# Hybrid GLA/DSA block with a PEER mixer: the dense stage's remaining dot products spread over 122 chunks instead of 112, and weighted three chunks ahead instead of five

## The chip, the core and the metric

The kernel runs on one core of a Trainium2 chip. A NeuronCore has TensorE (PE in the profile, with PEld for its weight loads), VectorE (DVE), ScalarE (ACT), GpSimd (POOL) and SyncE (SP), which issues most of the transfers. The metric is the time of one execution on the device in microseconds (us); the median of several runs counts.

## The reference

A decoder block for 512 tokens of width 1024: two token mixers (gated linear attention and sparse latent attention), merged, and then a PEER channel mixer. Only the last one matters here. Each token has 8 heads x 16 experts out of 16384, with gates:

```python
def block(inp):
    hx, ix, gx = inp
    u = expert_u[ix]
    v = expert_v[ix]
    a = jax.nn.gelu(jnp.einsum('td,thkd->thk', hx, u).astype(jnp.float32), approximate=False) * gx
    return jnp.einsum('thk,thkd->td', a.astype(hx.dtype), v)
```

So a token's output is the sum over its 128 experts of gelu(h . u_e) x gate_e x v_e.

## The kernel before

The PEER mixer is done in two ways. For the first half of the tokens (2 blocks of 128) the rows of `u` and `v` that a token picked are fetched by indirect DMA: `gather` (POOL, line 1009) brings 128 rows per step, one per token, of 8 KB (`u` and `v` side by side) in its last part; DVE takes the dot product (`dot`, line 1014) and one step later adds the weighted `v` half to the sum (`add`, line 1023). Its tiles `grow` are a ring of four. For the other 256 tokens (`NDT`) all 16384 experts are computed, 128 chunks (`P`) of 128 experts each:

- `dots_of` (line 931) makes one chunk's *dot*: h x u for 128 experts and 256 tokens, 8 products of `projT` (line 184) that TensorE runs as 16 matmuls, then Gelu on ACT (line 943) into a slot of `kept`, a ring of 48 (`AHEAD`). A load of `u` (line 937) brings two chunks, 1 MB, into the ring `up` of two slots.
- `weigh` (line 965) multiplies a chunk by its matrix of gates (DVE, line 972), which an earlier stage built; for the first 48 chunks that has been done there. The gates come in tiles of 8 chunks (`gtile`, line 961).
- The body of `dense` (line 950) loads `v` (line 979, two chunks, 1 MB, a ring of three), calls `weigh` for the chunk `LEAD` ahead, splits the weights and `v` into a high part (ACT, line 116) and the rest (DVE, line 117), `as` in a ring of four and `vs` in a ring of two, and adds the chunk's product: 4 accumulators x 3 matmuls of 128x512 (lines 186 to 188). Chunks 126 and 127 are multiplied together. Then come the dots that are due and one step of the gather (`pump`, at a rate of 1.05 per chunk).

48 dots are made before the dense stage starts; the other 80 inside it, by the rule in line 1002. At chunk 120 the tile `fx`, for the residual, takes a slot of the ring `up` (line 981). The order within an engine is set at build time by the framework's scheduler, from the order of the program and from `pace`, the DVE instruction after which a step of the gather may be placed. Each engine and each DMA queue runs its instructions in that order.

Of the kernel before, what the change touches and what calls it, by code (L numbers as in the profile page):

```python
# [20 lines left out]
P = 128  # L21
# [18 lines left out]
NE = 7  # L40
RATE_ADA, RATE_GLA, RATE_DSA, RATE_G, RATE_DENSE = 0.4, 0.75, 0.9, 1.0, 1.05
AHEAD = 48
LEAD = 5
DOTS = (8, 16)
RATE_SEL = 3.0
GB = 16
# [13 lines left out]
def hybrid_block_kernel(ctx, tc, x, c_col, w_ada, b_ada, b_col, g1_col, g2_col, wT, wN, wM, w_br, w_o,  # L60
# [50 lines left out]
    def behind(i):  # L111

        pace[0] = i.ins

    def split(hi, lo, src, eng=None, hi_eng=None):
        (hi_eng or nc.scalar.copy)(hi, src)  # L116
        i = (eng or nc.vector).tensor_tensor(lo, src, hi.bitcast(F32), op=ALU.subtract)  # L117
        if eng is not nc.gpsimd:
            pace[0] = i.ins
# [25 lines left out]
    def pump(n=1.0):  # L145

        if quiet[0]:
            return
        for b in background:
            b[2] += n * b[1]  # L150
            while b[2] >= 1:
                b[2] -= 1
                next(b[0], None)
# [28 lines left out]
    def mm(dst, a, b, first, last, **kw):  # L182
        if len(a) == 1:
            nc.tensor.matmul(dst, a[0], b[0], start=first, stop=last, **kw)  # L184
        else:
            nc.tensor.matmul(dst, a[0], b[0], start=first, stop=False, **kw)  # L186
            nc.tensor.matmul(dst, a[0], b[1], start=False, stop=False, **kw)  # L187
            nc.tensor.matmul(dst, a[1], b[0], start=False, stop=last, **kw)  # L188
# [723 lines left out]
    def finish(Tt, x2, peer):  # L912

        y = wp.tile([P, D], F32, name="fy", tag="raw", bufs=NRAW)
        ss = dn.tile([P, 2], F32, name="fs", bufs=2)
        for n in range(2):
            ns = slice(n * 512, (n + 1) * 512)
            nc.vector.tensor_tensor(y[:, ns], peer[n], gate2[:, ns], op=ALU.mult)
            nc.vector.tensor_tensor(x2[:, ns], x2[:, ns], y[:, ns], op=ALU.add)
            nc.scalar.activation(y[:, ns], x2[:, ns], AF.Square, accum_out=ss[:, n:n + 1])  # L920
        r = dn.tile([P, 1], F32, name="fr", bufs=2)
        nc.vector.tensor_tensor(r, ss[:, 0:1], ss[:, 1:2], op=ALU.add)
        rstd_of(r, r, D, 1)
        for n in range(2):
            ns = slice(n * 512, (n + 1) * 512)
            nc.vector.scalar_tensor_tensor(y[:, ns], x2[:, ns], r, fing[:, ns], op0=ALU.mult, op1=ALU.mult)
            nc.sync.dma_start(out[Tt * P:(Tt + 1) * P, ns], y[:, ns])
# [3 lines left out]
    def dots_of(ib):  # L931

        early = dn is None
        if ib % 2 == 0:
            pool, tag, bufs = ((wp, "w2", 2), (wp, "w2", 2), (hp, "hh", 1), (hp, "hl", 1))[ib // 2 % 4] if early else (dn, "up", 2)
            up[0] = pool.tile([P, 2, D], F32, name="up", tag=tag, bufs=bufs)
            nc.sync.dma_start(up[0], u_t[ib // 2])
        p = pmm(True)
        projT(p[:, :NDT], [up[0][:, ib % 2]], h2[1])
        a = kept[:, ib % AHEAD]  # L940
        d = built[0] if ib < AHEAD else 0
        if d < NDT:
            nc.scalar.activation(a[:, d:], p[:, d:NDT], AF.Gelu)  # L943
        if d:
            t = gb.tile([P, NDT], F32, name="dg", bufs=2)[:, :d]
            nc.scalar.activation(t, p[:, :d], AF.Gelu)
            behind(nc.vector.tensor_tensor(a[:, :d], a[:, :d], t, op=ALU.mult))
        made[0] += 1

    def dense():  # L950
        banks = [psc, psc, ptr, ptr]
        acc = [[banks[2 * i + n]() for n in range(2)] for i in range(NT - NG)]
        as4 = hp.tile([P, 4, 2, NDT], F32R, name="as", tag="hh")
        gts = []

        def load_g(c):

            if c < P // 8:
                pool, tag = ((dn, "gtile"), (hp, "hl"))[c % 2]
                gts.append(pool.tile([P, NDT // GB, 8, GB], F32, name="gtile", tag=tag))  # L960
                nc.sync.dma_start(gts[-1], gd[c - AHEAD // 8])

        load_g(AHEAD // 8)

        def weigh(ib):

            if ib < AHEAD:
                return
            if ib % 8 == 0:
                load_g(ib // 8 + 1)  # L970
            a3 = kept[:, ib % AHEAD].rearrange("p (b t) -> p b t", t=GB)
            behind(nc.vector.tensor_tensor(a3, a3, gts[ib // 8 - AHEAD // 8][:, :, ib % 8], op=ALU.mult))

        late_ops = []
        vb = x2 = None
        for ib in range(P):
            if ib % 2 == 0:
                vb = dn.tile([P, 2, D], F32, name="vb", bufs=3)
                nc.sync.dma_start(vb, v_t[ib // 2])
            if ib == P - 8:  # L980
                x2 = dn.tile([P, NT - NG, D], F32, name="fx", tag="up", bufs=2)
                for i in range(NT - NG):
                    nc.sync.dma_start(x2[:, i], x2d[NG + i])
            if ib + LEAD < P:
                weigh(ib + LEAD)
            a = as4[:, ib % 4]
            v = wp.tile([P, 2, D], F32R, name="vs", tag="w2", bufs=2)
            split(a[:, 0], a[:, 1], kept[:, ib % AHEAD])
            split(v[:, 0], v[:, 1], vb[:, ib % 2])
            a, v = [[t[:, 0], t[:, 1]] for t in (a, v)]  # L990
            late_ops.append((ib, a, v))
            stage[0] = ib
            if ib == P - 2:
                continue
            for i in range(NT - NG):
                ts_ = slice(i * P, (i + 1) * P)
                for n in range(2):
                    ns = slice(n * 512, (n + 1) * 512)
                    for jb, a, v in late_ops:
                        mm(acc[i][n], [t[:, ts_] for t in a], [t[:, ns] for t in v], jb == 0, jb == P - 1)  # L1000
            late_ops.clear()
            while made[0] < AHEAD + (ib + 1) * (P - AHEAD) // (P - 16) and made[0] < P:
                dots_of(made[0])
            pump()
        for i in range(NT - NG):
            finish(NG + i, x2[:, i], acc[i])
# [137 lines left out]
    made, built = [0], [0]  # L1144
# [21 lines left out]
    nc.sync.dma_start(gate2, gated[1])  # L1166
    background[:] = [[gat, RATE_DENSE, 0.0]]
    dense()
    drain(gat)

# [66 lines left out]
```

## Time and profile before

| | |
|---|---|
| median of 3 runs | 1853.64 us (1849.02 to 1855.12) |
| profiled execution: time, span | 1861.09 us, 1859.4 us |
| TensorE busy, weight loads busy | 1725.0 us (93%), 1466.6 us (79%) |
| DVE busy | 1432.8 us (77%) |
| ACT, POOL busy | 719.0 us (39%), 540.5 us (29%) |
| moved by DMA | 573.33 MB, mean 308 GB/s |
| dense stage, first to last matmul | 1202.95 to 1847.79 us |

The span is from the first to the last instruction; the time of the same execution is 1.7 us longer. Matmuls overlap each other in the records, so TensorE's work is better read from the distance between starts than from lengths.

### The profile page before, as it was taken

The page shows a single profiled execution, that of the slowest core. Times are in us where ns is not written, and L with a number is a line of the kernel's source. Part 1 is how long each engine was busy: PE and PEld are TensorE (multiplying, and loading weights), DVE is VectorE, ACT ScalarE, POOL GpSimd, SP SyncE. Part 2 cuts the span into 40 slices and gives each one's busy share as a digit, 9 for nine tenths or more (in the row PEclk, how much of TensorE's full clock was granted, in tenths as well). Part 3 has the DMA queues.
Part 4 walks back from the last instruction along what each step waited for, and adds up shares of the span by engine and source line. Part 5 has one row for each costly group of instructions (what it writes and reads, how often), then busy time and mean ns, then how long its engine had stood idle before and what let it go on. Part 6 is the DMA issues. An engine that isn't in the chain of part 4 may idle for free.

```text
span 1859.4 us, 25034 instructions
## 1 busy us (share of the span) xinstructions
PE 1725.0 (93%) x8898; PEld 1466.6 (79%) x8898; DVE 1432.8 (77%) x2985; ACT 719.0 (39%) x1694; POOL 540.5 (29%) x459
## 2 busy tenths in 40 slices
PE   6999999989899988988999789699999999999995
PEld 3888999878667877877778678588888888888874
DVE  5797645348999868757996999388878888788887
ACT  3644465332121134102144778243333434333343
POOL 0012000001454456653431666021222222222220
PEclk9999999989998999998999889899999999999998
DMA  7757556625786799996886999699999999999983
GB/s 289 281 182 272 187 188 213 231 88 204 245 303 237 284 353 387 381 383 233 294 286 222 345 315 367 246 416 401 403 401 404 397 404 412 395 405 410 393 354 122
DMA packets 145279, 573.33 MB, mean 308 GB/s; under 512 B 14449, under 2 KB 41201, under 8 KB 111106
## 3 DMA queue, kind: packets, MB, share of 16 engines
q1 hardware_dynamic: 89858, 303.28, 44.1%
q0 software_dynamic: 55296, 268.46, 37.4%
q8 instruction: 70, 1.15, 0.2%
q14 instruction: 55, 0.45, 0.1%
HBM read 553.86 MB, written 17.83 MB: 307 GB/s over the span
## 4 chain that ended last, share of the span: by engine, by line
issue 33%; PE 29%; DVE 15%; POOL 12%; DMA 8%; ACT 2%; SPq 0%; POOLq 0%; DVEq 0%; another core or an unknown queue 0%; ACTq 0%
POOL grow L1009 11%; PE pmm L184 8%; DMA grow<-rows,ids 4%; DVE grow L1014 3%; PE pmx L184 2%; PE pmm L187 2%; PE pmm L186 2%; PE pmm L188 2%; DVE gacc L1023 2%; DMA gd<-gs 2%; PE psc L898 2%; PE ptr L898 1%; DMA adaw<-w_ada 1%; PE pmx L187 1%; PE pmx L186 1%
## 5 line engine op out<-in xcount | busy, mean ns | idle before, releaser
L1009 POOL DMA_INDIRECT grow<-rows,ids x384 | 482.9, 1258 | 838.8 <-DVE h2n L1023 451.0
L184 PE MATMUL pmm<-h2h,up 128*128 128x256 f32 x2048 | 468.4, 381 | 5.0 <-ACT kept L943 3.1
L184 PEld LDWEIGHTS pmm<-h2h,up 128*128 128x128 f32 x2048 | 385.5, 191 | 59.3 <-ACT kept L943 3.9
L1014 DVE SCALAR_TENSOR_TENSOR grow<-grow,h2n 128x1024 f32<-128x1024 f32 x256 | 310.4, 1219 | 66.5 <-DMA grow<-rows,ids 65.2
L117 DVE TENSOR_TENSOR vs<-vb,vs 128x1024 fp32r<-128x1024 f32 x128 | 156.3, 1221 | 33.1 <-ACT vs L116 32.6
L1023 DVE SCALAR_TENSOR_TENSOR gacc<-grow,dots,gacc 128x1024 f32<-128x1024 f32 x127 | 161.9, 1275 | 15.1 <-DMA grow<-rows,ids 14.0
L1023 DVE SCALAR_TENSOR_TENSOR h2n<-grow,dots,h2n 128x1024 f32<-128x1024 f32 x127 | 162.5, 1280 | 0.0
L116 ACT CAST vs<-vb 128x1024 fp32r<-128x1024 f32 x128 | 133.3, 1042 | 6.0 <-PE ptr L188 3.9
L117 DVE TENSOR_TENSOR w<-raw,w 128x1024 fp32r<-128x1024 f32 x79 | 98.0, 1240 | 45.3 <-ACT w L116 45.0
L186 PE MATMUL psc<-vs,as 128*128 128x512 f32 x256 | 114.6, 454 | 14.5 <-ACT vs L116 14.5
L187 PE MATMUL psc<-vs,as 128*128 128x512 f32 x256 | 102.7, 401 | 10.4 <-DVE vs L117 10.4
L116 ACT CAST w<-raw 128x1024 fp32r<-128x1024 f32 x79 | 82.6, 1046 | 72.9 <-PE pmm L188 32.8
L184 PE MATMUL pmm<-hh,raw 128*128 128x256 f32 x416 | 99.8, 388 | 4.3 <-DVE bsg L689 2.1
L116 ACT CAST as<-kept 128x256 fp32r<-128x256 f32 x128 | 51.3, 403 | 133.7 <-PE ptr L187 128.9
L1062 ACT ACTIVATE dots<-dots 128x1 f32<-128x1 f32 x128 | 25.8, 202 | 198.2 <-DVE grow L1014 198.1
L188 PE MATMUL psc<-vs,as 128*128 128x512 f32 x256 | 101.0, 395 | 0.0
L187 PE MATMUL ptr<-vs,as 128*128 128x512 f32 x256 | 100.6, 393 | 0.0
L188 PE MATMUL ptr<-vs,as 128*128 128x512 f32 x256 | 100.6, 393 | 0.0
L186 PE MATMUL ptr<-vs,as 128*128 128x512 f32 x256 | 99.4, 393 | 0.0
L94 POOL TENSOR_TENSOR rs<-rs,mhalf 128x1 f32<-128x1 f32 (+1 forms) x24 | 18.1, 756 | 266.5 <-DVE rs L93 266.4
L184 PEld LDWEIGHTS pmm<-hh,raw 128*128 128x128 f32 x416 | 77.9, 193 | 17.3 <-DVE bsg L689 2.5
L117 DVE TENSOR_TENSOR as<-kept,as 128x256 fp32r<-128x256 f32 x128 | 53.4, 423 | 47.0 <-ACT as L116 46.9
(377 smaller groups left out, 3527.4 us busy)
## 6 DMA issues: line engine op xcount, KB each, us to landing
up<-u_t SPq DMA_DIRECT2D x64, 1024.0 KB
vb<-v_t SPq DMA_DIRECT2D x64, 1024.0 KB
raw<-wT SPq DMA_DIRECT2D x74, 512.0 KB
adaw<-w_ada SPq DMA_DIRECT2D x20, 1024.0 KB
raw<-wN SPq DMA_DIRECT2D x32, 512.0 KB
raw<-w_br SPq DMA_DIRECT2D x32, 512.0 KB
raw<-w_pq SPq DMA_DIRECT2D x32, 512.0 KB
gd<-gs SPq DMA_DIRECT2D x16, 640.0 KB
```

The costliest lines, as they stand in the source:

```text
L94: nc.gpsimd.tensor_tensor(dst, dst, mhalf[:, :w], op=ALU.pow)
L116: (hi_eng or nc.scalar.copy)(hi, src)
L117: i = (eng or nc.vector).tensor_tensor(lo, src, hi.bitcast(F32), op=ALU.subtract)
L184: nc.tensor.matmul(dst, a[0], b[0], start=first, stop=last, **kw)
L186: nc.tensor.matmul(dst, a[0], b[0], start=first, stop=False, **kw)
L187: nc.tensor.matmul(dst, a[0], b[1], start=False, stop=False, **kw)
L188: nc.tensor.matmul(dst, a[1], b[0], start=False, stop=last, **kw)
L898: nc.tensor.matmul(p[:, t], pm[:, t4_ + t], qm[:, t4_ + t], start=True, stop=True)
L1009: nc.gpsimd.indirect_dma_start(out=dst, out_offset=None, in_=table, in_offset=bass.IndirectOffsetOnAxis(ap=index[0][:, r:r + 1], axis=0))
L1014: nc.vector.scalar_tensor_tensor(u, u, 1.0, h2n[i], op0=ALU.mult, op1=ALU.mult, accum_out=dots[i][:, r:r + 1])
L1023: nc.vector.scalar_tensor_tensor(gacc, v, w, gacc, op0=ALU.mult, op1=ALU.add)
L1062: nc.scalar.activation(w, w, AF.Gelu)
```

## The change

Two lines change. `LEAD` is 3 instead of 5: a chunk is multiplied by its gates in the iteration three before its own. The number of dots that must be made after chunk `ib` is now 48 + (ib + 1) x 80 // 122 instead of // 112, so the last dot, 127, follows chunk 121 and not chunk 111.

```diff
-LEAD = 5
+LEAD = 3
...
-            while made[0] < AHEAD + (ib + 1) * (P - AHEAD) // (P - 16) and made[0] < P:
+            while made[0] < AHEAD + (ib + 1) * (P - AHEAD) // (P - LEAD - 3) and made[0] < P:
                 dots_of(made[0])
```

No instruction is added or removed. POOL's order is the same; that of PE, ACT, DVE and SP moves.

**ACT, the last chunks before the finish.** Each chunk is one cast of `as` and one of `vs`; each dot is one Gelu, `kept<-pmm`; L1062 and L1063 belong to the gather, L920 to the finish of a gathered block. Before:

```order
L116 CAST vs<-vb 128x1024
L1062 ACTIVATE dots_114<-dots_114 128x1
L1063 ACTIVATE dots_114<-dots_114,gate_112 128x1
L1062 ACTIVATE dots_114<-dots_114 128x1
L1063 ACTIVATE dots_114<-dots_114,gate_112 128x1
L116 CAST as<-kept 128x256
L116 CAST vs<-vb 128x1024
L116 CAST as<-kept 128x256
L116 CAST vs<-vb 128x1024
L920 ACTIVATE fy,fs<-fx 128x512 x2
L116 CAST as<-kept 128x256
L116 CAST vs<-vb 128x1024
```

ACT now, on the same last chunks:

```order
L1063 ACTIVATE dots_114<-dots_114,gate_112 128x1
L116 CAST as<-kept 128x256
L116 CAST vs<-vb 128x1024
L116 CAST as<-kept 128x256
L116 CAST vs<-vb 128x1024
L920 ACTIVATE fy,fs<-fx 128x512
L943 ACTIVATE kept<-pmm 128x256
L920 ACTIVATE fy,fs<-fx 128x512
L116 CAST as<-kept 128x256
L116 CAST vs<-vb 128x1024
L943 ACTIVATE kept<-pmm 128x256
L116 CAST as<-kept 128x256
```

Of before the rows hold no Gelu any more, since the last dot stands behind chunk 111. Now the Gelus of dots 126 and 127 (the two rows of L943) stand between the casts of chunks 122 and 124.

**SP, the last loads.** `up` is a block of `u` for two dots, `vb` of `v` for two chunks, `fx` the residual's tile. Before:

```order
L979 DMA vb<-v_t 128x2048 x2
L937 DMA up<-u_t 128x2048
L979 DMA vb<-v_t 128x2048
L937 DMA up<-u_t 128x2048
L979 DMA vb<-v_t 128x2048 x2
L983 DMA fx<-x2d_92 128x1024
L983 DMA fx<-x2d_93 128x1024
L979 DMA vb<-v_t 128x2048 x5
```

SP now, up to its last load:

```order
L979 DMA vb<-v_t 128x2048
L937 DMA up<-u_t 128x2048
L979 DMA vb<-v_t 128x2048 x2
L983 DMA fx<-x2d_92 128x1024
L983 DMA fx<-x2d_93 128x1024
L979 DMA vb<-v_t 128x2048
L937 DMA up<-u_t 128x2048
L979 DMA vb<-v_t 128x2048
```

The last block of `u`, which stood ahead of the loads of `fx`, now stands behind them and behind one more `vb`, with a single `vb` after it.

**DVE, from the split of chunk 119 on.** L972 is the weighing, L1014 and L1023 are the gather's dot and add, L918 begins the finish of the gathered block. Before:

```order
L117 TENSOR_TENSOR vs<-vb,vs 128x1024
L1014 SCALAR_TENSOR_TENSOR grow,dots_114<-grow,h2n_106 128x1024
L1023 SCALAR_TENSOR_TENSOR h2n_105<-grow,dots_114,h2n_105 128x1024
L1014 SCALAR_TENSOR_TENSOR grow,dots_114<-grow,h2n_106 128x1024
L1023 SCALAR_TENSOR_TENSOR h2n_105<-grow,dots_114,h2n_105 128x1024
L117 TENSOR_TENSOR as<-kept,as 128x256
L117 TENSOR_TENSOR vs<-vb,vs 128x1024
L1014 SCALAR_TENSOR_TENSOR grow,dots_114<-grow,h2n_106 128x1024
L1023 SCALAR_TENSOR_TENSOR h2n_105<-grow,dots_114,h2n_105 128x1024
L117 TENSOR_TENSOR as<-kept,as 128x256
L117 TENSOR_TENSOR vs<-vb,vs 128x1024
L1023 SCALAR_TENSOR_TENSOR h2n_105<-grow,dots_114,h2n_105 128x1024
```

DVE now, from the same split on:

```order
L117 TENSOR_TENSOR vs<-vb,vs 128x1024
L1014 SCALAR_TENSOR_TENSOR grow,dots_114<-grow,h2n_106 128x1024
L1023 SCALAR_TENSOR_TENSOR h2n_105<-grow,dots_114,h2n_105 128x1024
L1014 SCALAR_TENSOR_TENSOR grow,dots_114<-grow,h2n_106 128x1024
L1023 SCALAR_TENSOR_TENSOR h2n_105<-grow,dots_114,h2n_105 128x1024
L117 TENSOR_TENSOR vs<-vb,vs 128x1024
L1014 SCALAR_TENSOR_TENSOR grow,dots_114<-grow,h2n_106 128x1024
L1023 SCALAR_TENSOR_TENSOR h2n_105<-grow,dots_114,h2n_105 128x1024
L972 TENSOR_TENSOR kept<-kept,gtile 128x256
L117 TENSOR_TENSOR as<-kept,as 128x256
L972 TENSOR_TENSOR kept<-kept,gtile 128x256
L117 TENSOR_TENSOR as<-kept,as 128x256 x2
```

Of before the rows hold no weighing. Now two weighings, of chunks 124 and 125, stand here ahead of the split of `vs` of chunk 121, and those of 126 and 127 follow later. The gather's steps stand at nearly the same chunks as before.

## Rows read from the trace of the kernel before

**Rows 1.** Stretches: length, PE, PEld, DVE, ACT, POOL busy, PEclk, DMA share, GB/s.
```profile
1203.00:1793.80 590.80, 590.76 (x2649) 501.80 (x2650) 487.94 (x666) 228.04 (x546) 144.18 (x119) 0.99 0.99 402
1250.00:1750.00 500.00, 500.00 (x2256) 425.51 (x2256) 413.82 (x567) 193.23 (x463) 123.79 (x102) 1.00 0.99 403
1262.50:1275.00 12.50, 12.50 (x58) 10.68 (x57) 11.44 (x16) 4.64 (x12) 3.06 (x3) 1.00 0.85 343
1312.50:1325.00 12.50, 12.50 (x58) 10.65 (x57) 11.80 (x18) 5.10 (x11) 3.50 (x3) 1.00 1.01 425
1793.80:1847.80 54.00, 43.59 (x169) 32.27 (x167) 45.34 (x62) 22.57 (x46) 8.77 (x6) 0.94 0.52 199
...
1200.00:1212.50 12.50, 9.51 (x28) 7.18 (x29) 10.95 (x16) 4.95 (x10) 3.21 (x3) 0.63 1.01 423
1825.00:1827.00 2.00, 2.00 (x7) 1.52 (x6) 2.00 (x3) 1.45 (x2) 0.00 (x0) 0.50 0.25 33
```

**Rows 2.** Groups of 1250 to 1750: busy us, mean ns, idle us before them.
```profile
L184 PE MATMUL pmm<-h2h,up 128*128 128x256 f32 x1104 | 249.5, 379 | 0.0
L186 PE MATMUL psc<-vs,as 128*128 128x512 f32 x192 | 87.9, 458 | 0.0
L1023 DVE SCALAR_TENSOR_TENSOR h2n<-grow,dots,h2n 128x1024 f32<-128x1024 f32 x102 | 130.5, 1279 | 0.0
L1014 DVE SCALAR_TENSOR_TENSOR grow<-grow,h2n 128x1024 f32<-128x1024 f32 x101 | 123.1, 1219 | 24.5 <-DMA grow<-rows,ids 24.3
L117 DVE TENSOR_TENSOR vs<-vb,vs 128x1024 fp32r<-128x1024 f32 x97 | 118.4, 1220 | 23.9 <-ACT vs L116 23.4
```

**Rows 3.** All waits of PE from 1793.8 to 1847.8: total, times, longest.
```profile
PE psc L187 <- DVE vs L117: 10.4, 8, 6.3
```

**Rows 4.** PE in order of time: start, length, instruction, idle before it.
```profile
1202.95 1.22 PE L186 MATMUL psc<-vs,as 128*128 128x512 f32 x2 [14.53 <-ACT vs L116]
...
1211.73 3.61 PE L184 MATMUL pmm<-h2h,up 128*128 128x256 f32 x16
...
1748.43 3.61 PE L184 MATMUL pmm<-h2h,up 128*128 128x256 f32 x16
...
1754.61 0.39 PE L186 MATMUL psc<-vs,as 128*128 128x512 f32 x1
...
1757.33 3.61 PE L184 MATMUL pmm<-h2h,up 128*128 128x256 f32 x16
...
1793.71 0.39 PE L186 MATMUL psc<-vs,as 128*128 128x512 f32 x1
```

**Rows 5.** PE in order of time, the last chunks.
```profile
1800.59 0.50 PE L187 MATMUL psc<-vs,as 128*128 128x512 f32 x1 [0.23 <-DVE vs L117]
...
1808.44 0.50 PE L187 MATMUL psc<-vs,as 128*128 128x512 f32 x1 [0.99 <-DVE vs L117]
...
1821.68 0.80 PE L187 MATMUL psc<-vs,as 128*128 128x512 f32 x1 [6.31 <-DVE vs L117]
...
1826.97 0.49 PE L187 MATMUL psc<-vs,as 128*128 128x512 f32 x1
...
1830.76 0.50 PE L187 MATMUL psc<-vs,as 128*128 128x512 f32 x1 [0.79 <-DVE vs L117]
...
1836.59 0.50 PE L187 MATMUL psc<-vs,as 128*128 128x512 f32 x1 [0.33 <-DVE vs L117]
...
1847.40 0.39 PE L188 MATMUL ptr<-vs,as 128*128 128x512 f32 x1
```

**Rows 6.** The chain of waits: start, length, what.
```profile
1807.13 10.57 DMA grow<-rows,ids
```

**Rows 7.** Loads of `vb`: length in ns, first and last issue.
```profile
L979 SPq DMA_DIRECT2D vb<-v_t x64: 327/328/446, 1190.5 to 1825.7; - x64
```

**Rows 8.** Busy by stretch, after that last load.
```profile
1830.00:1830.50 0.50, 0.00 (x0) 0.00 (x0) 0.50 (x1) 0.50 (x2) 0.00 (x0) 1.00 0.00 0
```

**Rows 9.** Loads of `u` issued from 1250 to 1750.
```profile
up<-u_t SPq DMA_DIRECT2D x35, 1024.0 KB
```

## Prediction

> **What bounds the kernel now.** I read the busy time by stretch first, then the groups and waits of the dense stage, then TensorE's own line in order of time, then the chain of waits and the DMA.
>
> The stretches [rows 1] split the dense stage in two. From 1203 to 1793.8 us TensorE is busy all the time, and the DMA rings are busy to 0.99 at 402 GB/s: two resources are full at once. In the last 54 us TensorE falls to 43.6 of 54.0 us and the DMA to 0.52. A matmul's modelled length overlaps the next one's, so "busy" could hide gaps. The groups of 1250 to 1750 settle it: the matmuls of chunks and dots have 0.0 us of idle time before them, while DVE stood 24.3 us for gathered rows without TensorE feeling it [rows 2]. After 1793.8 the one PE wait is for DVE's `vs`, 10.4 us in 8 pieces [rows 3].
>
> By the Trainium skill (Perfetto Trace Analysis, Identifying the Most-Contended Engine) the share of weight loads tells how full TensorE is, not the share of matmuls. Here that is 425.5 of 500 us, 85%, which would leave TensorE headroom and make the DMA the tighter of the two; what that would make of the time is the first rival below.
>
> The pitch comes from TensorE in order of time [rows 4]. From a dot's start (1748.43) over the chunk behind it to the next chunk's start (1754.61) is 6.18 us; the chunk without a dot, 1754.61 to 1757.33, is 2.72 us; so a dot costs 3.46 us. The whole stage on TensorE alone is 128 x 2.72 + 80 x 3.46 = 625.0 us. It took from 1202.95 to 1847.79 [rows 4, 5], 644.8 us. Of the 19.8 us over:
> - 3.3 us lie at the start: two chunks from 1202.95 to the first dot at 1211.73, 8.78 us instead of 5.44, at a clock of 0.63 (between its two levels of 1.2 and 2.4 GHz) after 14.53 us of idleness [rows 1, 4].
> - 16.0 us lie in the last 14 chunks, 1793.71 to 1847.79: 54.1 us instead of 14 x 2.72 = 38.1. No dots are left there, so a chunk needs 2.72 us of TensorE but some 4 us of DVE (413.82 us for the 96 chunks of 500 us is 4.3, weighing included [rows 1]).
> - 0.5 us are spread.
>
> Behind DVE in that tail stands the gather: a fetch of 1807.13 takes 10.57 us in the chain of waits [rows 6], and TensorE stands 6.31 us until 1821.68 [rows 5]. Up to 1826.97 the next 12 matmuls take 5.29 us instead of 2.72, 2.6 us more, at a clock of 0.50, the 1.2 GHz level [rows 1, 5].
>
> **What the change does, by parts.**
>
> *The dots.* 80 dots of 3.46 us stay 80. Before, 5 follow every 7 chunks up to chunk 111 and 16 chunks stand bare; now 40 follow every 61 up to chunk 121 and 6 stand bare. In the dotted part a chunk cost 2.72 + 80/112 x 3.46 = 5.19 us and now costs 2.72 + 80/122 x 3.46 = 4.99. TensorE's sum is the same; what can go is the 16.0 us of the tail. There DVE set a pace of about 4 us; now TensorE sets 4.99 up to chunk 121, and DVE with its 4.3 us a chunk keeps ahead.
>
> *The new tail.* Chunks 122 to 127 are bare. The last four chunks of before, when the gather was over, ran from 1836.59 to 1847.79, 11.2 us against 10.9 at 2.72 [rows 5]. The first of the six still lie beside the finish of the gathered block on DVE, where one wait of 0.79 us stood before. I charge 1.0 us, between 0 and 2.
>
> *The last u load.* The ring `up` has two slots, and the load of `fx` takes one of them from chunk 120 on. So the u block of dots 126 and 127 is loaded only when dot 125 is through, and chunks 119 and 120 alone, 5.44 us, stand before dot 126. No dot has so short a cover in the trace, so I bound the wait. From below: the last v load, issued at 1825.7 into idle rings, has moved its bytes by 1830.0 [rows 7, 8], at most 4.3 us: no wait. From above: a fetch of 1 MB in full rings, 10.57 us [rows 6]: 5.1 us, and 2.6 more if the clock falls as it did at 1821. By then no fetch of the gather is left to issue and one or two are under way, so I take the value near the idle row, 0.5 us. A table of the Trainium skill (DMA: Bandwidth & Descriptors, Bandwidth) has 6.15 us for 1 MB by itself, which would be a wait of 0.7 us; the row here is shorter and decides.
>
> *The last gathered rows.* The fetch of row 127 leaves when DVE is done with row 124, about 7 us before dot 125 ends, and lands 10.57 us later, some 3.5 us after that end. Then DVE has a dot, an add and a split of `vs` (1.22, 1.28 and 1.22 us [rows 2]) and five operations of a quarter of their columns, an estimate of 5 us in all, before chunk 121, which starts 5.44 + 3.46 = 8.9 us after dot 125. That is just in time. Nothing to 3 us; I charge 1.0.
>
> *Three ahead instead of five.* The weighing of a chunk stays one DVE operation. It waits for the dot's Gelu, and DVE is in order, so one placed too early holds the next `vs`. Dot 127 is made in chunk 121 and weighed in chunk 124; five ahead would have weighed it in 122. The split behind it must wait for the chunk after the dot to leave its buffer, 2.72 us, and that covers the Gelu. Cost 0; with that cover gone it would be the Gelu's latency, twice.
>
> *Start and end.* The first chunks keep their order but for a dot that comes one chunk later; the finish behind the last matmul, 1847.8 to 1859.4, is untouched. Cost 0.
>
> **Sum:** 16.0 - 1.0 - 0.5 - 1.0 = 13.5 us less. Against the profiled execution: span 1859.4 to 1845.9, time 1861.09 to 1847.6. The median of the runs stands 7.45 us under the profiled time; I take the same amount off it: 1853.64 - 13.5 = **1840.1 us**. With every bound good it is 1853.64 - 16.0 = 1837.6, with every bound bad (2 + 5.1 + 2.6 + 3 = 12.7 off the 16.0) 1850.3.
>
> **Rivals.**
> - *The DMA becomes the bound.* The rings moved 403 GB/s x 500 us = 201.5 MB there, 35 u loads of 1.05 MB among it [rows 1, 9]. For the same chunks 35 become 32, so 198.4 MB, in 500 x 4.99/5.19 = 481 us: 412 GB/s. If 403 is all that they give, a chunk (2.06 MB) takes 5.11 us instead of 4.99, 14 us over 122 chunks, and 16.0 shrinks to 2: 1851.6, no change. For it: 0.99 busy and DVE's waits for rows. Against it: some stretches moved 425, and one with 343 was busy to 0.85 only, so part of what lacks is want of orders [rows 1]. By the skill's rule on weight loads, above, this is how it would go. 0.13.
> - *Part of the tail's stall comes back.* The late u load or a late row costs 7 to 8 us with a fall of the clock: 1847.5. 0.10.
> - *The stall belongs to the profiled execution.* If the 7.45 us by which that one is slower lie in the tail, 16.0 - 7.45 - 2.5 = 6 are to be had: 1847.6. 0.10.
> - *Slower: the two slots of `vs` run dry at each lone bare chunk.* Up to the last dot 42 chunks now have no dot behind them, 32 before. In the tail five bare chunks beside the great wait cost up to 0.99 us, 0.6 in the mean ((10.4 - 6.31 - 0.79 - 0.33)/5 [rows 3, 5]). 42 x 0.6 = 25 us less 13.5 gives 1865. From 13.5/42 = 0.32 us for each it is slower than before. Against it: some 27 bare chunks between 1250 and 1750 cost TensorE nothing [rows 2]. 0.06.
>
> **How the numbers follow.** The forecast keeps 0.61. About 0.3% (5.6 us) is what a measurement of this kernel can tell from no change. Faster by more: the forecast, two thirds of the second and third rivals and a little of the first, 0.75. Within: most of the first and the rest of those two, 0.18. Slower: the last rival and a bad end of the first, 0.07. The range has below it the good bound and the spread of the runs (1849.02 to 1855.12), above it the first rival: 1834 to 1852; the slower rival stays outside.
>
> **What would show it.** Right: the last dot some 16 us before the last matmul instead of 60; no PE wait for `vs` over 1 us in the stage; the clock at 1.00 to its end; the DMA near 410 GB/s until about 1810. Wrong: a PE wait for `up` of over 2 us before dot 126; DVE's waits for rows far above 24 us in 500 with PE waits behind them, the first rival; PE waits for `vs` at bare chunks, the last; or a stage that shrinks in the profile while the timed runs do not.

## The result and the profile after

The change took the kernel from a median of 1854.38 us (8 runs, 1849.02 to 1864.91) to 1843.57 us (8 runs, 1841.05 to 1847.23). The ratio is 0.9934, with a 95% interval of 0.9915 to 0.9953: 12.2 us less, between 8.7 and 15.8 (the two medians differ by 10.8). The forecast was 1840.1, and 13.5 us less.

The profiled execution of after takes 1842.98 us, 18.1 less than that of before. Part of that is not the change's: the dense stage begins at 1197.39 instead of 1202.95, while the two edited lines act inside it. (In eight profiles of the experiments below it begins between 1194.34 and 1208.88.) Within the stage, from first to last matmul, 644.84 became 632.27, 12.6 us less; behind it nothing moved. So the trace is read by the length of the stage.

The page of after: span, busy time by engine, and the slices with the clock and the DMA share.

```profile
span 1841.3 us, 25029 instructions
...
PE 1713.6 (93%) x8898; PEld 1459.3 (79%) x8898; DVE 1430.3 (78%) x2985; ACT 719.6 (39%) x1694; POOL 553.1 (30%) x459
...
PEclk9999999989998999989999979899999999999998
DMA  7848556625786799996876999699999999999992
```

Busy times and instruction counts tell nothing of a change that only reorders. The stretches do (columns as in [rows 1]):

```profile
1250.00:1750.00 500.00, 499.09 (x2248) 423.76 (x2247) 425.47 (x582) 199.28 (x475) 136.53 (x105) 1.00 1.00 411
...
1793.80:1829.50 35.70, 34.80 (x155) 28.44 (x153) 25.30 (x38) 13.06 (x25) 0.56 (x1) 1.00 0.31 116
```

Against [rows 1], mid-stage moves 411 GB/s instead of 403 with the rings busy to 1.00, and DVE does 425 us of work instead of 414 in the same 500: more chunks pass. The stretch from 1793.8 to the end is 35.7 us long instead of 54.0, TensorE is busy in 97% of it instead of 81%, and the clock stays at 1.00.

All waits of PE over the stage (total, times, longest), against [rows 3]:

```profile
PE psc L186 <- ACT vs L116: 14.4, 1, 14.4
PE pmm L184 <- DMA up<-u_t: 1.1, 2, 0.9
PE psc L187 <- DVE vs L117: 0.9, 1, 0.9
```

The first is the wait ahead of the stage, as before [rows 4]. Inside, the 10.4 us for `vs` are gone; two small waits for a `u` load and one for `vs` are left. TensorE in order of time shows them (start, length, instruction, idle before it):

```profile
1197.39 1.22 PE L186 MATMUL psc<-vs,as 128*128 128x512 f32 x2 [14.43 <-ACT vs L116]
...
1701.44 3.61 PE L184 MATMUL pmm<-h2h,up 128*128 128x256 f32 x16
1708.93 0.50 PE L187 MATMUL psc<-vs,as 128*128 128x512 f32 x1 [0.91 <-DVE vs L117]
1711.57 0.81 PE L184 MATMUL pmm<-h2h,up 128*128 128x256 f32 x3
...
1793.22 3.61 PE L184 MATMUL pmm<-h2h,up 128*128 128x256 f32 x16
1796.48 0.58 PE L186 MATMUL psc<-vs,as 128*128 128x512 f32 x1
...
1799.40 0.39 PE L186 MATMUL psc<-vs,as 128*128 128x512 f32 x1
...
1803.18 3.72 PE L184 MATMUL pmm<-h2h,up 128*128 128x256 f32 x16 [0.90 <-DMA up<-u_t]
1806.55 0.59 PE L186 MATMUL psc<-vs,as 128*128 128x512 f32 x1
...
1809.51 3.61 PE L184 MATMUL pmm<-h2h,up 128*128 128x256 f32 x16
...
1829.27 0.39 PE L188 MATMUL ptr<-vs,as 128*128 128x512 f32 x1
```

The rows at 1793.22, 1803.18 and 1809.51 are dots 125, 126 and 127. From the last of them to the end (1829.66) is 20.15 us, where 3.46 + 6 x 2.72 = 19.78 would do. Chunk 120 starts at 1799.40, so dot 126 could have started at 1802.12 and is 1.06 late. From 1701.44 to 1711.57 lie a dot and two chunks, 10.13 us instead of 8.90.

The account of the stage against the minimum of 625.0 us that the prediction worked out, in us:

| over the minimum | before | after |
|---|---|---|
| start, at a low clock | 3.3 | 3.4 |
| waits in mid-stage (two after: `u` at 1236.79, `vs` at 1708.93) | 0 | 1.7 |
| the end (after: late `u` load 1.2, last six chunks 0.4) | 16.0 | 1.6 |
| spread | 0.5 | 0.6 |
| sum | 19.8 | 7.3 |

### The profile page after: what moved, and what is told of

Same layout as the page of the kernel before. It is cut to its first block, busy times and chain, and to the rows that moved or that the text cites. A ratio compares the mean times of both kernels' runs of the same rounds, so it can differ in the third digit from the quotient of the medians.

```text
span 1841.3 us, 25029 instructions
## 1 busy us (share of the span) xinstructions
PE 1713.6 (93%) x8898; PEld 1459.3 (79%) x8898; DVE 1430.3 (78%) x2985; ACT 719.6 (39%) x1694; POOL 553.1 (30%) x459
## 3 DMA queue, kind: packets, MB, share of 16 engines
q8 instruction: 70, 1.15, 0.3%
## 4 chain that ended last, share of the span: by engine, by line
PE 36%; issue 28%; DVE 14%; POOL 10%; DMA 8%; ACT 2%; POOLq 0%; SPq 0%; DVEq 0%; ACTq 0%
PE pmm L184 12%; POOL grow L1009 10%; DMA grow<-rows,ids 5%; PE pmx L184 3%; DVE grow L1014 3%; PE pmm L188 2%; PE pmm L186 2%; PE pmm L187 2%; DVE gacc L1023 2%; DMA gd<-gs 2%; PE psc L898 2%; PE ptr L898 1%; PE pmx L187 1%; PE pmx L186 1%; PE pmx L188 1%
## 5 line engine op out<-in xcount | busy, mean ns | idle before, releaser
L1009 POOL DMA_INDIRECT grow<-rows,ids x384 | 495.7, 1291 | 805.6 <-DVE h2n L1023 423.7
L1014 DVE SCALAR_TENSOR_TENSOR grow<-grow,h2n 128x1024 f32<-128x1024 f32 x256 | 310.8, 1221 | 91.2 <-DMA grow<-rows,ids 90.7
L1023 DVE SCALAR_TENSOR_TENSOR gacc<-grow,dots,gacc 128x1024 f32<-128x1024 f32 x127 | 162.5, 1280 | 14.6 <-DMA grow<-rows,ids 14.2
L1023 DVE SCALAR_TENSOR_TENSOR h2n<-grow,dots,h2n 128x1024 f32<-128x1024 f32 x127 | 162.8, 1282 | 0.0
L1062 ACT ACTIVATE dots<-dots 128x1 f32<-128x1 f32 x128 | 25.9, 202 | 223.1 <-DVE grow L1014 222.8
L94 POOL TENSOR_TENSOR rs<-rs,mhalf 128x1 f32<-128x1 f32 (+1 forms) x24 | 18.1, 754 | 267.2 <-DVE rs L93 267.1
L893 ACT ACTIVATE qm<-eq,gaT 128x128 f32<-128x128 bf16 x256 | 79.3, 391 | 14.2 <-DVE eq L887 14.1
```

Source lines behind the costliest of these rows:

```text
L893: nc.scalar.activation(qm[:, t], e[:, t // 2, :, t % 2], AF.Copy, scale=gaT[:, t0 + t:t0 + t + 1])
L1009: nc.gpsimd.indirect_dma_start(out=dst, out_offset=None, in_=table, in_offset=bass.IndirectOffsetOnAxis(ap=index[0][:, r:r + 1], axis=0))
L1014: nc.vector.scalar_tensor_tensor(u, u, 1.0, h2n[i], op0=ALU.mult, op1=ALU.mult, accum_out=dots[i][:, r:r + 1])
L1023: nc.vector.scalar_tensor_tensor(gacc, v, w, gacc, op0=ALU.mult, op1=ALU.add)
L1062: nc.scalar.activation(w, w, AF.Gelu)
```

## The experiments

**Theory A:** the 16.0 us were DVE and the gather setting the pace of 14 chunks that had no dots. Spreading the dots puts TensorE's work beside that DVE work; the spread alone carries the gain, weighing three ahead gives nothing, and what is left over comes from the order of the last loads. Each expectation names the rival that it is set against. Stage means first to last dense matmul.

**1. The spread alone** (against after).

```diff
-LEAD = 3
+LEAD = 5
-            while made[0] < AHEAD + (ib + 1) * (P - AHEAD) // (P - LEAD - 3) and made[0] < P:
+            while made[0] < AHEAD + (ib + 1) * (P - AHEAD) // (P - 6) and made[0] < P:
```

> The dots spread over 122 chunks, but weighing five chunks ahead as before. Theory A (the gain is the dots that now cover the bare chunks of the tail, three-ahead is worth nothing): dense stage from first to last matmul 632 us as with the whole change, within 1.5 us, time 12 us under before. Rival (three-ahead is needed): the weighing of chunks 125 to 127 stands on DVE before its dot is made, DVE waits for the Gelu and TensorE for vs; 2 to 6 us of PE waits for vs beyond the 0.9 us of the whole change, stage 634 to 638 us.

Measured: 1848.15 us (10 runs) beside 1858.61 for before on the same chip, ratio 0.9938 (0.9918 to 0.9958), the same gain as the whole change; stage 633.3. The waits of PE over the stage have no `vs` among them; the timeline shows the one for `u`:

```profile
1807.41 5.41 PE L184 MATMUL pmm<-h2h,up 128*128 128x256 f32 x16 [2.22 <-DMA up<-u_t]
1812.47 0.58 PE L186 MATMUL psc<-vs,as 128*128 128x512 f32 x1
```

So weighing five ahead would have done. The late `u` load, issued at 1799.77, costs more here: 2.22 us of wait, and then 5.06 us from the dot's start to the next chunk, where dot 125 of after took 3.26; from 1808.41 to 1812.47 the granted clock is 0.58. From dot 125 to dot 127 that makes 4.2 us over the minimum.

**2. Three ahead alone** (against before).

```diff
-LEAD = 5
+LEAD = 3
```

> Weighing three chunks ahead, the dots over 112 chunks as before. Theory A: nothing changes: dense stage 643 to 646 us, tail of 14 chunks about 54 us with PE waits of 10 us for vs, time within 3 us of before. Rival (three-ahead carries part of the gain): stage shorter by 3 us or more.

Measured: 1860.1 us (10 runs), ratio 1.0016 (0.9994 to 1.0039), no change; stage 645.7. From 1797 to 1852 PE's waits, and the longest of them:

```profile
PE psc L187 <- DVE vs L117: 10.9, 8, 4.4
```

```profile
1823.59 0.50 PE L187 MATMUL psc<-vs,as 128*128 128x512 f32 x1 [4.36 <-DVE vs L117]
```

That is the tail of [rows 3] again, 10.9 us in 8 pieces. Of the two edits the spread carries the gain.

**3. `fx` later** (against after): the residual's tile takes its slot of `up` at chunk 122 instead of 120, behind the last `u` load.

```diff
-            if ib == P - 8:
+            if ib == P - 6:
```

> The whole change, and the tile fx taken from the ring of u at chunk 122 instead of 120, behind the last dot, so that the last u block goes to a slot that is free one block earlier. If the ring slot causes the PE wait for the last u load (0.90 us with the whole change), that wait is 0 and the stage about 1 us shorter, 631 us; the time moves by less than can be measured. If the full DMA rings cause it, a wait of 0.5 us or more stays.

Measured: the last `u` load leaves at 1776.89, some 17 us earlier in its stage than in after, and PE waits for nothing in the whole stage, which takes 629.7. The time is 1845.97 us (9 runs), ratio 0.9932 (0.9903 to 0.9961): the 2.6 us of the stage against after are too few to be measured. Mid-stage, by stretch:

```profile
1250.00:1750.00 500.00, 500.00 (x2254) 424.96 (x2253) 425.79 (x582) 198.45 (x476) 135.49 (x106) 1.00 1.00 412
```

This is the best version of the study by its stage, and the row settles a question of the prediction: TensorE issues without a gap, and its weight loads are busy to 425 of 500 us, the same 85% as in [rows 1]. The Trainium skill (Perfetto Trace Analysis, Identifying the Most-Contended Engine) takes that share, together with the share of peak arithmetic, as the measure of headroom; here the trace does not bear that out: at 85% no engine or transfer kept TensorE waiting, and there was no idle time left to gain.

**4. Before, without the gather's last 12 rows** (against before).

```diff
-        for r in range(P):
+        for r in range(P - 12):
```

> Before, with the last 12 rows of the second gathered block left out (its output is then not the reference's), so that the gather ends some 11 chunks earlier. Theory A (DVE's work for the gather, and its late rows, set the pace of the bare chunks): the 14 chunks from 112 on take 38 to 41 us instead of 54, PE waits for vs under 2 us, time 13 to 16 us under before. Rival (a bare chunk is held by its own split, ACT then DVE through a ring of two): the waits of 0.2 to 1.0 us per chunk stay, the tail takes 45 us or more.

Measured (one run): 1839.96 us, stage 630.1 instead of 644.8, with the dots where they stood before. From the last dot to the end, by stretch:

```profile
1779.97:1827.30 47.33, 47.33 (x209) 38.74 (x207) 26.81 (x34) 20.64 (x30) 0.00 (x0) 1.00 0.34 123
```

TensorE is busy all the time, though 16 chunks still stand bare; the minimum for a dot and 16 chunks is 46.98. So the tail's 16.0 us were the gather's last rows, their work on DVE and their late arrival together; the ring of two slots of `vs` alone costs the bare tail nothing. How the 16.0 divide between DVE's work and the wait for rows stays open.

**5. 117 chunks** (against after).

```diff
-            while made[0] < AHEAD + (ib + 1) * (P - AHEAD) // (P - LEAD - 3) and made[0] < P:
+            while made[0] < AHEAD + (ib + 1) * (P - AHEAD) // (P - 11) and made[0] < P:
```

> The whole change with the dots over 117 chunks, so that 11 chunks stand bare and the gather's last rows fall on some four of them. Theory A (each bare chunk beside the gather costs DVE's 4 us instead of TensorE's 2.72, and late rows on top): stage between the two kernels, 634 to 640 us, PE waits for vs of 2 to 7 us after the last dot. Rival (the tail costs only when the rings empty of dots for all of 16 chunks): 632 us, as with 122.

Measured (one run): 1849.28 us, stage 634.5; the waits of PE, one of 0.46 us in mid-stage and the other three behind the last dot:

```profile
PE psc L187 <- DVE vs L117: 3.9, 4, 2.0
```

The last dot starts at 1796.20 and the stage ends at 1835.97: 39.77 us, 6.4 over the minimum. With 16 bare chunks it was 16.0, with 6 it is 0.4. So fewer bare chunks beside the gather cost less, by three points, of which this one is a single run.

**6. 124 chunks** (against after): the last dots lose their cover, and are weighed as soon as their Gelu is there.

```diff
-            while made[0] < AHEAD + (ib + 1) * (P - AHEAD) // (P - LEAD - 3) and made[0] < P:
+            while made[0] < AHEAD + (ib + 1) * (P - AHEAD) // (P - 4) and made[0] < P:
```

> The whole change with the dots over 124 chunks, weighing still three ahead: dot 127 is made after chunk 123 and weighed in front of the split of chunk 124. Theory A: the cover is gone, DVE and ACT wait for the Gelu of dot 127 in front of that split and TensorE waits 1 to 4 us for vs behind the last dot; stage 633 to 636 us, no gain over 122. Rival (the weighing never holds anything): no PE wait there, stage 630 to 632 us.

Measured (one run): 1850.15 us, stage 634.3, the number expected for another reason. DVE does stand for the Gelu, twice:

```profile
1820.01 0.42 DVE L972 TENSOR_TENSOR kept<-kept,gtile 128x256 f32<-128x256 f32 x1 [1.57 <-ACT kept L943]
...
1826.20 0.42 DVE L972 TENSOR_TENSOR kept<-kept,gtile 128x256 f32<-128x256 f32 x1 [1.57 <-ACT kept L943]
```

but PE waits for nothing behind the last dots. Its waits are in mid-stage:

```profile
1304.54 0.50 PE L187 MATMUL psc<-vs,as 128*128 128x512 f32 x1 [2.01 <-DVE vs L117]
...
1614.28 0.50 PE L187 MATMUL psc<-vs,as 128*128 128x512 f32 x1 [1.54 <-DVE vs L117]
```

The mechanism expected was wrong: behind the Gelu DVE stands, TensorE does not. From dot 125 to the end this run is only 0.4 us over the minimum, the last `u` load included, where after is 1.6; what makes its stage longer are the waits in mid-stage, where the order hardly differs. One run does not tell whether 124 brings these waits or whether they come and go.

**7. The gather at 1.15 rows per chunk** (against after): the same transfers in fewer chunks, so a greater need of DMA per chunk.

```diff
-RATE_ADA, RATE_GLA, RATE_DSA, RATE_G, RATE_DENSE = 0.4, 0.75, 0.9, 1.0, 1.05
+RATE_ADA, RATE_GLA, RATE_DSA, RATE_G, RATE_DENSE = 0.4, 0.75, 0.9, 1.0, 1.15
```

> The whole change with the gather at 1.15 steps a chunk instead of 1.05: about 2.16 MB for a chunk of 4.99 us, 434 GB/s, over the 425 seen at best in 12.5 us. If the DMA rings are as near to their limit as that says, TensorE waits for vs many times between 1250 and 1750, the DMA stands at 415 to 425 GB/s, and the stage takes 8 to 20 us longer, 640 to 652 us. If the rings have more to give, 632 us as before and over 425 GB/s.

Measured (one run): 1885.77 us, stage 663.6, 31 us over after, more than expected; and the rings gave less, not more. The stretch, and the waits of 1250 to 1750:

```profile
1250.00:1750.00 500.00, 480.13 (x2109) 402.99 (x2108) 419.95 (x572) 190.35 (x466) 136.50 (x108) 0.98 0.99 406
```

```profile
DVE grow L1014 <- DMA grow<-rows,ids: 70.8, 54, 3.3
...
PE psc L187 <- DVE vs L117: 19.7, 10, 3.2
```

The chain is rows late, DVE late, `vs` late, TensorE stopped. Some matmuls behind such a stop show a fall of the clock, as here, where the pitch is 0.42 us instead of 0.23:

```profile
1458.52 0.79 PE L187 MATMUL psc<-vs,as 128*128 128x512 f32 x1 [3.18 <-DVE vs L117]
1459.12 0.63 PE L188 MATMUL psc<-vs,as 128*128 128x512 f32 x1
1459.54 0.63 PE L186 MATMUL psc<-vs,as 128*128 128x512 f32 x1
```

Which resource was out? Not plainly the DMA. The ring of `grow` has four slots, and a fetch leaves only when DVE's `add` has freed one. First POOL's waits for that, then two fetches on POOL and two dots on DVE:

```profile
POOL grow L1009 <- DVE h2n L1023: 358.5, 107, 5.4
```

```profile
1442.01 0.95 POOL L1009 DMA_INDIRECT grow<-rows,ids  x1 [3.60 <-DVE h2n L1023]
1448.38 1.69 POOL L1009 DMA_INDIRECT grow<-rows,ids  x1 [5.43 <-DVE h2n L1023]
```

```profile
1445.68 1.22 DVE L1014 SCALAR_TENSOR_TENSOR grow<-grow,h2n 128x1024 f32<-128x1024 f32 x1 [1.94 <-DMA grow<-rows,ids]
1454.90 1.23 DVE L1014 SCALAR_TENSOR_TENSOR grow<-grow,h2n 128x1024 f32<-128x1024 f32 x1 [1.83 <-DMA grow<-rows,ids]
```

Behind the dot at 1445.68 comes the `add` that releases the fetch at 1448.38, 2.70 us later; that fetch brings the row for the dot three steps on. The fetch at 1442.01 is the one that the dot at 1454.90 waits for. In after a fetch takes 11.2 us in the median (from issue to landing). An estimate from these rows: a row every (2.70 + 11.2) / 3 = 4.63 us is all that four slots give. Experiment 7 had 108 fetches in 500 us, one in 4.63, where 1.15 per chunk of 4.99 asks for one in 4.34; after asks for one in 4.75. From a fetch to its dot the median is 11.2 us in experiment 7 and 11.7 in after, so the fetches did not become slower. The change runs close to an edge, and by these rows it is that of the gather's ring of four; a deeper ring was not run.

**8. `fx` later, without the gather's last 12 rows** (against after): the floor.

```diff
-            if ib == P - 8:
+            if ib == P - 6:
...
-        for r in range(P):
+        for r in range(P - 12):
```

> The whole change with fx taken at chunk 122 and the last 12 rows of the second gathered block left out (its output is then not the reference's): neither the last u load nor late rows are left. Theory A: stage 628 to 630 us, which is 128 x 2.72 + 80 x 3.46 = 625.0 us and the 3.3 us of the slow start, no PE wait over 0.3 us in the last 60 us; so what the gather still costs the changed kernel is under 2 us. Rival (another limit stands behind): 631 us or more.

Measured (one run): 1841.72 us, stage 629.9, with one PE wait of 0.2 us. Experiment 3 with all its rows has 629.7: once dots stand beside them, the gather's last rows cost TensorE nothing that the stage shows.

## Why the prediction was right, and where its terms were off

The direction, the place and the mechanism held. Of the 13.5 us forecast, 12.6 came in the profiled stage and 12.2 (8.7 to 15.8) in the timed runs. The median, 1843.57, lies 3.5 us over the forecast of 1840.1: the medians differ by 10.8 instead of 13.5, and before itself came out 0.74 higher than the three runs shown. That the sum of terms came within 1 us of the stage is in part luck: the new tail and the last rows were charged 2.0 and took 0.4, the last `u` load and the dotted part were charged 0.5 and took 2.9.

- *The dots* (16.0): right. Experiment 1 has the gain by the spread alone, experiment 4 shows whose stall it was, and experiment 5, with 11 bare chunks, lies between.
- *The new tail* (charged 1.0): measured 0.4.
- *The last u load* (charged 0.5, the value near the idle row): measured 1.2. This step took the wrong neighbour. The chain of waits of after shows the load by itself:

```profile
1796.86 6.28 DMA up<-u_t
```

  6.28 us lie between the bounds of 4.3 and 10.57. The load that gave the lower bound had moved its bytes 4.3 us after its issue; this one had not. The last 2 us of it still show a thin stream, at a DMA share of 0.13 (columns as in [rows 1]):

```profile
1800.86:1802.86 2.00, 1.42 (x7) 0.84 (x5) 1.98 (x3) 0.69 (x3) 0.00 (x0) 1.00 0.13 49
```

  Why it ended so slowly is open. The Trainium skill's 6.15 us for 1 MB (DMA: Bandwidth & Descriptors, Bandwidth; measured there for transfers issued by GpSimd), which the prediction set aside for its own row, is 0.13 from the measurement in after; in experiment 1 it was 7.6 us from the issue at 1799.77 to the dot at 1807.41. Experiment 3 shows that the slot that `fx` takes was the cause, as the prediction said.
- *The last gathered rows* (charged 1.0): measured 0 on TensorE in after. On DVE row 127 is late, yet the split for chunk 121 is done at 1806.12, and chunk 121 starts at 1806.55. But the late `u` load had moved that start back by 1.2 us.

```profile
1800.88 1.22 DVE L1014 SCALAR_TENSOR_TENSOR grow<-grow,h2n 128x1024 f32<-128x1024 f32 x1 [3.86 <-DMA grow<-rows,ids]
...
1804.90 1.22 DVE L117 TENSOR_TENSOR vs<-vb,vs 128x1024 fp32r<-128x1024 f32 x1
```

  Experiment 3 has no late `u` load. There the same split ends at 1800.99, behind the start of chunk 121, and from that start to dot 127 it is 3.17 us instead of the 2.92 of a chunk behind a dot: "just in time" was 0.25 us late.

```profile
1799.76 1.23 DVE L117 TENSOR_TENSOR vs<-vb,vs 128x1024 fp32r<-128x1024 f32 x1
```

```profile
1800.50 0.58 PE L186 MATMUL psc<-vs,as 128*128 128x512 f32 x1
...
1803.67 3.61 PE L184 MATMUL pmm<-h2h,up 128*128 128x256 f32 x16
```

- *Three ahead* (0): right; experiments 1 and 2 put a number to it from both sides, and experiment 6 shows that even with the cover gone it is DVE that stands, not TensorE.
- *The dotted part* (charged nothing): the step that failed, by 1.7 us, 0.5 at a `u` load and 1.2 at a `vs`. The prediction had DVE "keep ahead" from its mean of 4.3 us a chunk. The mean holds, but in after DVE waits twice as long for rows, in 50 waits instead of 18. The waits of DVE from 1250 to 1750, where [rows 2] has 24.3 us for them:

```profile
DVE grow L1014 <- DMA grow<-rows,ids: 47.8, 50, 4.4
```

  The longest of these reached TensorE at 1708.93. The chain of waits of after leads there from a fetch of 11.83 us over DVE, whose own order of time shows the wait and the late split:

```profile
1692.40 11.83 DMA grow<-rows,ids
```

```profile
1704.25 1.23 DVE L1014 SCALAR_TENSOR_TENSOR grow<-grow,h2n 128x1024 f32<-128x1024 f32 x1 [4.44 <-DMA grow<-rows,ids]
...
1707.66 1.21 DVE L117 TENSOR_TENSOR vs<-vb,vs 128x1024 fp32r<-128x1024 f32 x1
```

  In experiments 1 and 3 the longest wait for a row is 3.5 and 3.3 us, and none reached TensorE. The spread is not needed for it: in experiments 2 and 4, with the dots spaced as in before, waits for a row of 4.70 and 4.82 us stopped TensorE for 0.28 and 0.40 us, and from 1250 to 1750 DVE waited 32.2 and 31.2 us for rows. How much of the 1.7 us belongs to the change is open.

The rivals. *The DMA as the bound* did not come true: the rings gave the 411 to 412 GB/s that the prediction had worked out as the need, so 403 was not all that they give. Experiment 7 fell behind at 406, but by the estimate there the gather's own ring accounts for the shortfall; how much full DMA rings lengthen a fetch was not tested. *A late load or row with a fall of the clock* came true in small: 1.2 us in after, with no fall of the clock, and 4.2 in experiment 1, with one; not 7 to 8. *The stall belongs to the profiled execution* is refuted: it left 6 us to be had, and the timed interval begins at 8.7. *The ring of `vs` dry at each lone chunk* is refuted: one wait of 0.91 us in the stage, and experiment 4 shows the ring of two keeping pace. One sign did not come: the DMA was to stay near 410 GB/s until about 1810, but it moved 174 from 1799 to 1804, since the last gathered row was in by 1800.88.

## What to carry to other kernels

Where one engine is full in one stretch and idles in the next behind another, moving its work from the full stretch into the idle one gains the idle time at no cost in instructions; the gain is read from the idle stretch (pitch per step against the minimum), not from the shares of the whole. Before counting on it, work out what the other resources must now give in the stretch that becomes shorter, and test that edge by pushing it a little further; a ring that is refilled only when a slot comes free has an edge of its own, its slots against the time of one fetch. And look at the last load of each ring: a tile that borrows a slot near the end delays the load behind it. In experiment 3 one line took that wait away.

## What the runs showed of the hardware

- Over 500 us the DMA moved 403 GB/s in before, 411 and 412 in after and experiments 1 and 3, and 406 in experiment 7, which had more to fetch per chunk; the 425 of a 12.5 us stretch [rows 1] was not held over 500 us in any of them. The DMA share was 0.99 at 403 and at 406 and 1.00 at 411: the share did not tell how much more they would give.
- What a late row costs comes on top of the row: experiment 7's stage is 31 us longer, of which PE's waits for `vs` in 1250 to 1750 are 19.7 and matmuls at half clock behind some of them a further part.
- TensorE's clock fell behind stops of 2.22 us (experiment 1, granted 0.58 from 1 us after the restart) and 3.18 us (experiment 7, granted 0.50), and the matmuls behind the stop of 0.90 us in after kept their pace, granted 1.00. The length of the stop did not decide it alone: in experiment 7 the 2.5 us behind a stop of 2.19 us (1317.58) were granted 0.54, and those behind one of 2.22 us 1.00, with a pitch of 0.23 us:

```profile
1424.87 0.50 PE L187 MATMUL psc<-vs,as 128*128 128x512 f32 x1 [2.22 <-DVE vs L117]
1425.20 0.39 PE L188 MATMUL psc<-vs,as 128*128 128x512 f32 x1
1425.44 0.40 PE L186 MATMUL psc<-vs,as 128*128 128x512 f32 x1
```
